# The last unit's last two gate tiles move from the pool that is replaced to the pool that stays

## The chip, the cores and the metric

The kernel runs on one core of a Trainium2 chip. The metric is the device time of one execution, in microseconds (us). The core has five engines that work side by side, each on its own queue in order: TensorE (PE in the profile, with its weight loads as PEld), VectorE (DVE), ScalarE (ACT), GpSimd (POOL) and SyncE (SP). Here SP issues the loads of the weights, and POOL issues most other DMA transfers. Tiles live in SBUF; matmuls write to PSUM.

## The reference

What is computed is an encoder trunk of two layers on 512 positions of 1024 channels. Each layer projects its normalized input once, for three branches and for a gate per branch, then merges, projects back and runs an MLP:

```python
for l in range(DEPTH):
    xn = rms_norm(x, ln1[l])
    z = xn @ w_in[l]
    a_q, a_i, a_ff, a_fb, a_g, b_u, b_v, c_q, c_k, c_v, gz = jnp.split(z, offsets, axis=-1)
    o_a = hgrn2_bidirectional(a_q, a_i, a_ff, a_fb, lower[l])
    ...
    y_b = spatial_gating(jax.nn.gelu(b_u), jax.nn.gelu(b_v), w_s[l], b_s[l])
    ...
    y_c = window_attention(qh, kh, vh, sink[l])
    gates = jax.nn.sigmoid(gz.reshape(bsz, s_len, N_BRANCH, D_MODEL))
    merged = (gates[:, :, 0] * (y_a @ w_br[l, 0]) + gates[:, :, 1] * (y_b @ w_br[l, 1])
              + gates[:, :, 2] * (y_c @ w_br[l, 2]))
    x = x + merged @ w_out[l]
    x = x + jnp.square(jax.nn.relu(rms_norm(x, ln2[l]) @ w_up[l])) @ w_down[l]
return rms_norm(x, final_norm)
```

Branch A is a gated linear recurrence in both directions, branch B mixes positions within blocks of 128 by a matrix `w_s` per group, branch C is attention in a window with rotary positions. All values are float32.

## The kernel before, in words

**Precision.** A product is made of three matmuls in the type fp32r: the high parts of both factors, and the high part of each with the low part of the other. So each 128x1024 piece of a weight goes through three steps: a DMA from DRAM into a raw tile (`wr`, or `wq` in the units), a cast by ACT at L224 (`wh`), and a subtraction by DVE at L225 (`wl`).

**The units.** In each layer three blocks of the input projection are done by Strassen's method, with seven products in place of eight (`seven`, L434). These are the units u = 0, 1, 2. Unit 0 makes the values of branch A and one input of branch B (`vt`, `bv`). Units 1 and 2 make gates: `on_gate(0)` and `on_gate(1)`. Within a unit the products run in the order 1, 2, 6, 7, 5, 4, 3, and each gives two tiles in PSUM (`gA`, `gB`, `gC`). As a product ends, `on` (L868) copies it to a tile `zt`, adds it to one, or, for the last, `P1653`, takes its tanh straight from PSUM (L875). A finished gate tile of 128x512, 256 KB, is written to a scratch tensor `thd` in DRAM by a DMA on POOL's queue (`keep`, L866) and read back much later, in the merge.

**The pools.** `zt` and the shifted inputs `xs` live in the pool `G`, the units' raw weights in the pool `wq`. Behind the units both are ended (L903, L904) and two others take their room: `Y1` (`yh`) and `br`, in which the attention stage has nearly all its tiles (`ex`, `at`, `key`, `qt`, `kt`, `yb`, the masks `am` and `cmask`). A tile of the new pool can be written only when the tiles of the old one that lay there have been read. The pool `sb` stays throughout. It holds, under the tag `l` with eight slots, tiles of several stages, and among them the four small tables `wst` (the mixing matrices), `bsb` (their bias), `cos` and `sin` (L918 to L922). The slots of a tag are given out in the order in which the program asks for tiles.

**The order.** The program does not fix the order of instructions on an engine by hand: a scheduler builds it from the order in the text, from priorities and from its own estimate of when each thing is ready. So a change of one tile's place can move instructions at other places.

**Behind the units** PE goes on with the projection `f` (L229 to L231: 24 matmuls for each 512 columns) and then `q`, while ACT and DVE start branch A: `key` (L622) and `qt` (L614) for the matmuls `at` (L600). Branch B comes in between: the matmuls `mx` (L944) multiply `wst` with `bv`, DVE adds `bsb` (`yb`, L947), multiplies by `bu` (L948), and ACT and DVE split the result (`yh`, L287, `yl`, L288). `mx` has two PSUM tiles in turn. Branch C later multiplies by `cos` and `sin`, which DVE first scales by the row norm (L989). In the first layer the mask `am` is loaded too, in two halves (L912), and cast to bytes by DVE (L913).

## Time and profile before

| | us |
|---|---|
| median of three runs | 1692.38 |
| lowest and highest of them | 1691.42, 1693.87 |
| the profiled execution | 1692.82 |
| its span | 1690.9 |
| outside the span | 1.9 |
| PE busy | 1675.8 |
| DVE busy | 1287.7 |
| ACT busy | 1010.1 |
| bytes moved by DMA | 195.83 MB, 116 GB/s on average |

The granted clock of TensorE is full (0.999) over the whole span. The span starts at 0 us; the units of the first layer end at 161.6 us, those of the second at 1003 us. In a row of the timeline the first number is the start, the second the duration, and in brackets stands how long the engine had been idle before and what ended that. In a row of waits stand the total, the number of times and the longest. In a row of DMA issues stand how many, the size of each, and the median time from issue to landing.

### The profile page before, as it was taken

The page shows a single profiled execution, that of the slowest core. Times are in us where ns is not written, and L with a number is a line of the kernel's source. Part 1 is how long each engine was busy: PE and PEld are TensorE (multiplying, and loading weights), DVE is VectorE, ACT ScalarE, POOL GpSimd, SP SyncE. Part 2 cuts the span into 40 slices and gives each one's busy share as a digit, 9 for nine tenths or more (in the row PEclk, how much of TensorE's full clock was granted, in tenths as well). Part 3 has the DMA queues.
Part 4 walks back from the last instruction along what each step waited for, and adds up shares of the span by engine and source line. Part 5 has one row for each costly group of instructions (what it writes and reads, how often), then busy time and mean ns, then how long its engine had stood idle before and what let it go on. Part 6 is the DMA issues. An engine that isn't in the chain of part 4 may idle for free.

```text
span 1690.9 us, 21905 instructions
## 1 busy us (share of the span) xinstructions
PE 1675.8 (99%) x8034; PEld 1403.3 (83%) x8034; DVE 1287.7 (76%) x2011; ACT 1010.1 (60%) x1714; POOL 111.0 (7%) x169
## 2 busy tenths in 40 slices
PE   9999999999999999999999999999999999999998
PEld 8888888888888888888788888888887888888886
DVE  7996998685656768686989869986846577585967
ACT  7566678765235554545765768698752355545464
POOL 1011000110200000000010110000002000000000
PEclk9999999999999999999999999999999999999999
DMA  8342222132645333332423422212227353232311
GB/s 326 112 149 88 89 77 69 57 113 94 227 153 187 100 100 100 100 109 91 137 91 122 161 92 76 99 44 88 94 81 252 129 186 100 100 113 87 125 63 50
DMA packets 58138, 195.83 MB, mean 116 GB/s; under 512 B 7504, under 2 KB 7888, under 8 KB 58032
## 3 DMA queue, kind: packets, MB, share of 16 engines
q1 hardware_dynamic: 47520, 160.23, 27.9%
q0 software_dynamic: 10368, 33.96, 5.7%
q8 instruction: 63, 1.03, 0.2%
q14 instruction: 43, 0.35, 0.1%
q10 hardware_dynamic: 144, 0.26, 0.0%
HBM read 175.54 MB, written 18.87 MB: 115 GB/s over the span
## 4 chain that ended last, share of the span: by engine, by line
PE 78%; DVE 9%; ACT 7%; issue 5%; DMA 1%; POOL 1%; POOLq 0%; DVEq 0%; ACTq 0%
PE up L229 7%; PE up L231 7%; PE up L230 7%; PE dA L447 3%; PE dA L445 3%; PE dA L446 3%; PE wo L280 2%; PE wo L281 2%; PE wo L279 2%; PE dC L446 2%; PE dC L445 2%; PE dC L447 2%; DVE ex L642 2%; PE at L600 1%; PE po L1084 1%
## 5 line engine op out<-in xcount | busy, mean ns | idle before, releaser
L224 ACT CAST wh<-wq 128x1024 fp32r<-128x1024 f32 x201 | 211.6, 1053 | 200.2 <-PE dA L446 48.3
L225 DVE TENSOR_TENSOR wl<-wq,wh 128x1024 fp32r<-128x1024 f32 x201 | 244.9, 1222 | 110.2 <-ACT wh L224 109.0
L225 DVE TENSOR_TENSOR wl<-wr,wh 128x1024 fp32r<-128x1024 f32 x166 | 203.5, 1226 | 142.3 <-ACT wh L224 135.7
L224 ACT CAST wh<-wr 128x1024 fp32r<-128x1024 f32 x166 | 174.2, 1050 | 223.3 <-PE up L230 73.4
L229 PE MATMUL up<-xh,wh 128*128 128x512 f32 x512 | 199.3, 389 | 0.0
L230 PE MATMUL up<-xl,wh 128*128 128x512 f32 x512 | 199.2, 389 | 0.0
L231 PE MATMUL up<-xh,wl 128*128 128x512 f32 x512 | 198.2, 389 | 0.0
L231 PEld LDWEIGHTS up<-xh,wl 128*128 128x128 f32 x512 | 96.1, 188 | 20.0
L230 PEld LDWEIGHTS up<-xl,wh 128*128 128x128 f32 x512 | 96.1, 188 | 19.9
L229 PEld LDWEIGHTS up<-xh,wh 128*128 128x128 f32 x512 | 96.1, 188 | 19.8
L445 PE MATMUL dA<-wh,sh 128*128 128x512 f32 x256 | 99.7, 389 | 0.0
L446 PE MATMUL dA<-wh,sh 128*128 128x512 f32 x256 | 99.6, 389 | 0.0
L447 PE MATMUL dA<-wl,sh 128*128 128x512 f32 x256 | 92.9, 389 | 0.0
L642 DVE TENSOR_TENSOR ex<-ex 128x512 f32<-128x512 f32 x112 | 74.8, 685 | 2.5 <-ACT key L622 2.4
L600 PE MATMUL at<-qt,kt 128*128 128x128 f32 x448 | 63.4, 275 | 1.7 <-ACT yh L287 1.7
L600 PEld LDWEIGHTS at<-qt,kt 128*128 128x128 f32 x448 | 58.5, 191 | 3.7 <-ACT yh L287 1.8
L614 ACT ACTIVATE qt<-ex 128x512 f32<-128x512 f32 x56 | 37.6, 672 | 35.2 <-DVE ex L642 19.8
L446 PEld LDWEIGHTS dA<-wh,sh 128*128 128x128 f32 x256 | 48.1, 188 | 10.0
L447 PEld LDWEIGHTS dA<-wl,sh 128*128 128x128 f32 x256 | 48.1, 188 | 9.9
L445 PEld LDWEIGHTS dA<-wh,sh 128*128 128x128 f32 x256 | 48.0, 188 | 9.9
L287 ACT CAST sh<-sf 128x512 fp32r<-128x512 f32 x64 | 39.7, 620 | 21.9 <-DVE sf L410 16.6
L230 PE MATMUL gz<-xl,wh 128*128 128x512 f32 x128 | 50.8, 397 | 0.0
(413 smaller groups left out, 4339.7 us busy)
## 6 DMA issues: line engine op xcount, KB each, us to landing
wr<-in_ws_dram SPq DMA_DIRECT2D x166, 512.0 KB, 3.3
wq<-in_ws_dram SPq DMA_DIRECT2D x117, 512.0 KB, 4.3
thd<-zt POOLq DMA_DIRECT2D x32, 256.0 KB, 2.5
th<-thd POOLq DMA_DIRECT2D x32, 256.0 KB, 3.1
mgd<-mg POOLq DMA_DIRECT2D x16, 256.0 KB, 2.3
mB<-mgd POOLq DMA_DIRECT2D x16, 256.0 KB, 4.6
xt<-in_xt_dram SPq DMA_DIRECT2D x8, 256.0 KB, 7.3
mcd<-th POOLq DMA_DIRECT2D x8, 256.0 KB, 3.4
```

The lines of the kernel that those rows point to most:

```text
L224: cast_i[0] = nc.scalar.copy(hi, raw)
L225: nc.vector.tensor_tensor(lo, raw, hi.bitcast(F32), ALU.subtract)
L229: nc.tensor.matmul(pt, whi, xhi, start=first, stop=False)
L230: nc.tensor.matmul(pt, whi, xlo, start=False, stop=False)
L231: return nc.tensor.matmul(pt, wlo, xhi, start=False, stop=last)
L287: nc.scalar.copy(hi, src)
L445: nc.tensor.matmul(pt, xh[:, t], hi[:, c], start=start and k == 0, stop=False, skip_group_check=True)
L446: nc.tensor.matmul(pt, xl[:, t], hi[:, c], start=False, stop=False, skip_group_check=True)
L447: return nc.tensor.matmul(pt, xh[:, t], lo[:, c], start=False, stop=k == 3, skip_group_check=True)
L600: nc.tensor.matmul(pt[:, c], kk(st), qq[:, c], start=True, stop=True)
L614: nc.scalar.activation(qt.rearrange(shp, b=nb, h=2), e_q, AF.Exp)
L642: nc.vector.tensor_tensor(o_ap, o_ap, ap_of(ex, i_, [[istep, 2]] + z), ALU.add)
```

## The change

The two tiles of the product `P1653` of the last unit (`i` is 1) are asked for under the tag `l`, which lies in the pool `sb`, and no longer under `zt`, which lies in the pool `G`. The unit before keeps `zt`. Nothing else in the text differs:

```diff
@@ -871,7 +871,7 @@
                     w[which, p] = T("zt", "zt")
                     A.copy(w[which, p], pt)
                 elif which == "P1653":
-                    z = T("zt", "zt")
+                    z = T("l" if i else "zt", "zt")
                     A.activation(z, pt, AF.Tanh, scale=sc[:, 4 + p:5 + p])
                     keep(z, p, 1)
                 else:
```

Both tiles are 128x512 in float32, and both tags hold such tiles. The four tables stand later in the program and take the slots of `l` behind the two tiles. Both kernels have the same instructions in number; their order differs between the first gate unit and the merge of each layer, and nowhere else.

POOL's queue in the first layer, one piece of the difference, at the end of the units (`zt_1217` and `zt_1219` are the tiles of the product before the last, `zt_1369` and `zt_1372` those of the last):

```order
 L866 DMA thd<-zt_1217 128x512
 L866 DMA thd<-zt_1219 128x512
+L919 DMA wst_1394<-in_wst_dram 128x512
+L920 DMA bsb_1395<-in_bsb_dram 128x512
 L866 DMA thd<-zt_1369 128x512
+L921 DMA cos_1396<-in_rope_dram 128x512
+L922 DMA sin_1397<-in_rope_dram 128x512
 L866 DMA thd<-zt_1372 128x512
 L916 DMA cmask_1392<-in_cmask_dram 128x384
```

Before, the four loads stood far ahead, in the first unit; now they stand among the last four gate tiles. The second layer has the same order.

PE's queue in the first layer, within the projection `f` behind the units, one piece of the difference (`mx_1579` and `mx_1587` are the first two groups of branch B's mixing, `at_1408` is branch A's first):

```order
 L229 MATMUL f_346_1668<-xh_189,wh_1664 128x512
+L944 MATMUL mx_1579<-wst_1394,bv_792 128x128
+L944 MATMUL mx_1579<-wst_1394,bv_794 128x128
+L600 MATMUL at_1408<-qt_1403,kt_1406 128x128 x4
+L944 MATMUL mx_1579<-wst_1394,bv_612 128x128
+L944 MATMUL mx_1579<-wst_1394,bv_614 128x128
+L944 MATMUL mx_1587<-wst_1394,bv_792 128x128
+L944 MATMUL mx_1587<-wst_1394,bv_794 128x128
+L944 MATMUL mx_1587<-wst_1394,bv_612 128x128
+L944 MATMUL mx_1587<-wst_1394,bv_614 128x128
 L230 MATMUL f_346_1668<-xl_190,wh_1664 128x512
```

The eight `mx` matmuls of the first two groups stood before in pairs at four places within the units; `at_1408` stood some 20 rows later, among the `mx` of the fourth group. The third group (`mx_1595`) now follows seven rows of `f`, two groups of `at` and one more row of `f`.

DVE's queue in the first layer at the same place. Before:

```order
L225 TENSOR_TENSOR wl_1706<-wr_1703,wh_1705 128x1024
L947 TENSOR_TENSOR yb_1584<-mx_1579,bsb_1395 128x512
L947 TENSOR_TENSOR yb_1592<-mx_1587,bsb_1395 128x512
L948 SCALAR_TENSOR_TENSOR bu_430<-yb_1584,bu_430 128x512
L788 TENSOR_TENSOR z_338_1629<-f_342_1636,rb_399 128x512
L948 SCALAR_TENSOR_TENSOR bu_432<-yb_1592,bu_432 128x512
L615 TENSOR_TENSOR qt_1403<-qt_1403,q_494 128x512
L642 TENSOR_TENSOR ex_1092<-ex_1092 128x2x256
L913 CAST amask_t<-am_1384 128x448
L913 CAST amask_t<-am_1387 128x448
```

And in the changed kernel, from the second row behind `wl_1706` on:

```order
L642 TENSOR_TENSOR ex_1092<-ex_1092 128x2x256
L913 CAST amask_t<-am_1384 128x448
L913 CAST amask_t<-am_1387 128x448
L642 TENSOR_TENSOR ex_1092<-ex_1092 128x2x256
L788 TENSOR_TENSOR z_338_1629<-f_342_1636,rb_399 128x512
L225 TENSOR_TENSOR wl_1739<-wr_1736,wh_1738 128x1024
L615 TENSOR_TENSOR qt_1425<-qt_1425,q_494 128x512
L642 TENSOR_TENSOR ex_1092<-ex_1092 128x2x128x2
L989 TENSOR_TENSOR cos_1396<-cos_1396,rb_399 128x512
L642 TENSOR_TENSOR ex_1092<-ex_1092 128x2x128x2
L989 TENSOR_TENSOR sin_1397<-sin_1397,rb_399 128x512
L947 TENSOR_TENSOR yb_1584<-mx_1579,bsb_1395 128x512
```

`yb` was first behind the last `wl` of the units; now branch A's first steps, the two casts of `am` and the two products of `cos` and `sin`, which stood in the first unit before, come ahead of it. On SP's queue the two loads of `am` now stand ahead of the third weight load behind the units (`wr_1773`), and not behind it.

## The prediction

> **What bounds the kernel now.** I read the page first, for the engine that is full.

> ```profile
> PE 1675.8 (99%) x8034; PEld 1403.3 (83%) x8034; DVE 1287.7 (76%) x2011; ACT 1010.1 (60%) x1714; POOL 111.0 (7%) x169
> ```

> TensorE is the bound: 1675.8 of 1690.9 us. The change removes no instruction, so it can gain only what TensorE waits, 15.1 us in all, and of that only what lies where the order of work differs: about 100 to 425 us (first layer) and 925 to 1273 us (second). So next the view of waits, for PE alone, in these two stretches:

> ```profile
> PE at L600 <- ACT yh L287: 1.7, 1, 1.7
> PE pT L1079 <- ACT yc L1086: 0.9, 1, 0.9
> ...
> PE po L1084 <- ACT pT L1080: 0.6, 1, 0.6
> PE kT L657 <- ACT at L620: 0.6, 1, 0.6
> PE f L229 <- DVE gz L967: 0.4, 1, 0.4
> PE gA L445 <- ACT wh L224: 0.3, 1, 0.3
> PE pT L1079 <- ACT yc L1086: 0.2, 1, 0.2
> PE yC L279 <- DVE mC L1147: 0.2, 1, 0.2
> ```

> The first two are the first layer, the other six the second: 2.6 + 2.3 = 4.9 us. This is the most that better order can bring here. The first, 1.7 us, is the one at the edit. The timelines of PE, ACT, DVE, POOL and SP around it (start, us, what; in brackets the idle time before and who ended it), and last the chain of waits:

> ```profile
> 161.61 0.39 PE L229 MATMUL f<-xh,wh 128*128 128x512 f32 x1
> ...
> 170.91 1.72 PE L944 MATMUL mx<-wst,bv 128*128 128x128 f32 x14
> 174.31 0.46 PE L600 MATMUL at<-qt,kt 128*128 128x128 f32 x2 [1.68 <-ACT yh L287]
> ...
> 162.57 1.05 ACT L224 CAST wh<-wr 128x1024 fp32r<-128x1024 f32 x1
> 169.28 1.06 ACT L622 ACTIVATE key<-ex 128x1024 f32<-128x1024 f32 x1 [5.66 <-DMA thd<-zt]
> ...
> 169.35 1.29 DVE L947 TENSOR_TENSOR yb<-mx,bsb 128x512 f32<-128x512 f32 x2 [4.47 <-DMA thd<-zt]
> ...
> 158.17 1.16 POOL L866 DMA_DIRECT2D thd<-zt  x2 [4.34 <-ACT zt L881]
> 162.12 1.22 POOL L866 DMA_DIRECT2D thd<-zt  x2 [2.79 <-ACT zt L875]
> ...
> 158.54 6.69 SPq L200 DMA_DIRECT2D wr<-in_ws_dram  x3
> 169.23 0.81 SPq L912 DMA_DIRECT2D am<-in_amask_dram  x2
> ...
> 162.80 6.18 DMA thd<-zt
> ```

> The units' last product (gA) ends where f begins, at 161.61. The last two gate tiles are issued to DRAM at 162.12 and 162.7, and the second lands 6.2 us after its issue, at 168.98; until then ACT, DVE, POOL and SP all stand, because their next instructions write into the pool that replaces the one where these tiles lie. TensorE lives on 41 matmuls of f (161.61 to 170.91, 0.227 us each) and the mx matmuls, and then runs dry for 1.68 us: mx needs yb to empty its PSUM tile, the at matmuls need qt.

> **The change part by part.**

> *The wait that goes.* In the new order the attention stage waits for the tiles of the product before (issued at 158.17 and 158.7) and no longer for the last two. The transfers issued from 158.0 to 159.5 landed in:

> ```profile
> thd<-zt POOLq DMA_DIRECT2D x2, 256.0 KB, 3.5
> ```

> So the wait ends near 162 us, not at 168.98. The key instruction of ACT is then released not by the transfer but by the cast at 162.57: it can start some 5 us sooner than 169.28. Thus qt, issued as the second after it, is ready near 165. If nothing else is late, the whole 1.68 us gap goes.

> *What is moved into its place.* wst, bsb, cos and sin take slots of the tag "l" behind the two tiles, and are now issued among the last gate tiles. The first of them today:

> ```profile
> wst<-in_wst_dram POOLq DMA_DIRECT2D x1, 256.0 KB, 3.0
> ```

> All four are issued from 38 us on, where nothing waits for them, and cost nothing. Now 4 x 256 KB = 1 MB comes into the busiest stretch. In turn the mx matmuls that stood in the units, 8 in each layer, move behind f's 34th matmul:

> ```profile
> 106.28 0.60 PE L944 MATMUL mx<-wst,bv 128*128 128x128 f32 x4
> 106.64 0.71 PE L447 MATMUL gA<-wl,xs 128*128 128x512 f32 x2
> 107.19 0.39 PE L445 MATMUL gA<-wh,xs 128*128 128x512 f32 x1
> ```

> From 106.28 to 107.19 are 0.91 us, of which the two gA matmuls take 2 x 0.227, so two mx matmuls (four rows) cost 0.457 us; eight are 1.83 us. TensorE works as much as before: the units end 1.83 us sooner (gA at 159.8) and f's stretch is 1.83 us longer. There are ten switches fewer between the two number formats on PE (302, not 312); since mx rows take 0.114 us there and 0.123 us in the block of 14 at 170.91 (1.72/14), I price them at nothing to 0.1 us and take 0.1.

> *Does wst come in time?* PE reaches the first mx 34 x 0.227 = 7.7 us after 159.8, at 167.5. wst is issued behind the transfer of 156.9 (158.7 less 1.83), near 157.5. The stretch's own prices are:

> ```profile
> wr<-in_ws_dram SPq DMA_DIRECT2D x3, 512.0 KB, 5.3
> thd<-zt POOLq DMA_DIRECT2D x4, 256.0 KB, 5.3
> am<-in_amask_dram SPq DMA_DIRECT2D x2, 224.0 KB, 2.6
> ```

> At 5.3 us it lands by 162.8, with 4.7 us to spare. Price: zero; without this cover each us is one on the path.

> *The tightest link: am.* In DVE's new queue the two casts of am stand ahead of both cos and sin products and of yb; yb frees the PSUM that mx's second half needs. PE gets there after 34 f matmuls (167.5), eight mx (1.83), three groups of at (0.94 each, from the 16 rows in 2.04 us below), and eight f matmuls (1.8): 174.0.

> ```profile
> 174.31 2.04 PE at L600 x16
> 173.43 0.68 DVE L615 TENSOR_TENSOR qt<-qt,q 128x512 f32<-128x512 f32 x1
> 174.03 0.68 DVE L642 TENSOR_TENSOR ex<-ex 128x512 f32<-128x512 f32 x1
> 174.63 0.68 DVE L913 CAST amask_t<-am 128x448 uint8<-128x448 f32 x2
> 175.24 1.21 DVE L225 TENSOR_TENSOR wl<-wr,wh 128x1024 fp32r<-128x1024 f32 x1
> ```

> From am's landing to the end of the first yb DVE has the two casts (0.61), seven products of 128x512 at a pitch of 0.60 (4.2), the wl (1.13) and yb itself (0.68): 6.6 us. So am must land by 167.4. It is issued when gA's end (159.8) and the earlier gate tiles (160.5 to 161) have cleared, so it has 6.4 to 6.9 us. Lower bound of its landing: the 2.6 us of today, a stall of nothing. Upper: all that is under way then.

> ```profile
> 160.00:165.00 5.00, 5.00 (x23) 4.13 (x22) 2.45 (x2) 2.42 (x3) 1.08 (x2) 1.00 0.87 291
> ```

> The last three numbers are the granted clock, the share of the DMA engines and GB/s: in this stretch they are 87% busy at 291 GB/s, about 334 if full. On SP's own queue some 1.1 MB go up to am's end (the rest of one wr, another wr, am). If SP's and POOL's queues halve the rate, that takes 1.1 MB / 167 GB/s = 6.6 us, landing near 167.5 with a little for the start. If am waits for every byte under way, 2.0 to 2.6 MB at 291 GB/s, it takes 7 to 9 us: 168 to 170. I take a stall of 0.5 us, near the first (one wr of 512 KB takes 5.3 us here, and so do the gate tiles, which go in pairs of 512 KB: neither queue is preferred), with 0 and 2.6 as ends. [...]

> *cos and sin* are needed by DVE at about 171; issued near 161, they have 10 us. POOL's queue holds wst, bsb, tile, cos, sin, tile, cmask: at 167 GB/s its six times 256 KB and 192 KB from 157.5 on take 10.6 us, so sin comes before 167 and cmask last, which this row needs first at 226 us:

> ```profile
> L1053 DVE CUSTOM_DVE_ANT_0 sc<-sc,cmask,snk_t x64: 462/544/619, 225.6 to 1232.8; 128x256 f32<-128x256 f32 x32, 128x384 f32<-128x384 f32 x32
> ```

> Both cost nothing.

> *The second layer* loses and gains nothing at this place:

> ```profile
> 1005.00:1010.00 5.00, 5.00 (x24) 4.14 (x23) 2.35 (x3) 1.64 (x3) 0.54 (x1) 1.00 0.78 285
> ...
> ACT qt L614 <- DMA thd<-zt: 3.4, 1, 3.4
> ```

> ACT waits 3.4 us for the tiles there too, but PE never stops: it has no am in the way and more matmuls in hand. f still has wst some 3 us ahead of its need.

> *The other gaps* (0.92 and the 2.3 us of layer 2) come from ACT's order among small steps. DVE has 24 to 25 of 25 us in use from 175 to 250, so its sooner start (some 3 us after the 1.4 us for cos and sin that now fall here) may clear the 0.92; a new order can as well make gaps of 0.2 to 0.9. I put their sum at zero, with -3.2 and +1.5 as ends.

> **Sum:** -1.68 + 0.5 - 0.1 = -1.3 us. Profiled execution 1692.8 to 1691.5; it stood 0.4 above the median of 1692.38, so the median goes to 1691.1.

> **The rivals.**

> A, *the sooner start carries on*: the transition's gap goes whole and the small gaps of the reordered stretches with it. For it: DVE is full behind the transition and gets 3 us ahead. Against: the second layer's gaps are ACT's and lie 100 us and more behind. 4.9 us less at most, three quarters of it likely: 1692.4 - 3.8 = 1688.6.

> B, *the wait only changes its name*: am, or the wr in front of it, comes 1.2 us later than I put it, and PE's 1.68 us stand at mx in place of at. For it: 1 MB more in a stretch with the engines 87% busy. Against: half the rate suffices. 1692.3.

> C, *slower: the late loads hold DVE's queue*. One mechanism: the am casts hold all that stands behind them on DVE, cos, sin and yb, and PE stands at mx's second half. It decides from a landing of am at 169.1 (1.68 us past 167.4). What the engines moved from 157 to 170 us, and the gate tiles' landing over the whole run:

> ```profile
> DMA packets 754, 2.65 MB, mean 204 GB/s; under 512 B 112, under 2 KB 112, under 8 KB 752
> ...
> thd<-zt POOLq DMA_DIRECT2D x32, 256.0 KB, 2.5
> ```

> With all 2.6 MB ahead of it at this mean it takes 12.7 us from 161: 173.7, a stall of 6.3, net +4.6; at 291 GB/s 9 us, net +0.9. The middle: 1695.1. [...]

> **How the numbers follow.** Forecast 0.43, A 0.18, B 0.22, C 0.17. The time is the forecast's, 1691.1, its own range 1690.0 to 1692.0. The whole range goes from 1688.0 (all but A's last us) to 1694.8 (half of C), leaving out some 0.15. About 0.2%, 3.4 us, is what a measurement tells from no change: faster than 1689.0 is most of A and a little of the forecast's tail, 0.16; slower than 1695.8 some half of C with new gaps added, 0.11; the rest, 0.73, is the same.

> **What would show it.** Right: ACT's key starts by 164, behind a cast and not behind thd; no gap ahead of at; a gap under 1 us, if any, ahead of the mx matmuls of the third tile, behind DVE; am landing 6 to 7 us after issue; units ending 1.8 us sooner in both layers. B shows a gap of 1.2 to 2.2 us at that mx, C of over 2; A shows none there and none at pT near 272. Wrong altogether: PE stopping at the first mx for wst, new gaps over 1 us in the second layer, or a time outside 1688.0 to 1694.8.

## The result, and the profile after

The changed kernel is slower: 1694.78 us (1692.68 to 1696.54, 20 executions) beside 1691.79 us of the kernel before (1690.48 to 1693.87, 20 executions). The ratio is 1.0018, with a 95% interval of 1.0011 to 1.0024. The forecast was 1691.1, within 1690.0 to 1692.0.

The page of the changed kernel, first line of the engines:

```profile
PE 1677.9 (99%) x8034; PEld 1404.5 (83%) x8034; DVE 1291.1 (76%) x2011; ACT 1010.8 (60%) x1714; POOL 111.7 (7%) x169
```

TensorE does the same 8034 matmuls and is busy 2.1 us longer. The waits of PE in the two stretches where the order differs, first layer, then second:

```profile
PE at L600 <- DVE qt L615: 2.3, 1, 2.3
PE mx L944 <- DVE yb L947: 1.0, 1, 1.0
...
PE at L600 <- ACT on L701: 1.4, 1, 1.4
PE f L229 <- DVE gz L967: 0.4, 1, 0.4
PE gz L229 <- DVE gz L967: 0.2, 1, 0.2
```

In the first layer 3.3 us stand where 2.6 stood, at other places; in the second 2.0 where 2.3 stood. The timelines of PE, ACT, DVE and SP behind the units of the first layer show what happened:

```profile
167.10 0.60 PE L944 MATMUL mx<-wst,bv 128*128 128x128 f32 x4
167.54 1.06 PE L600 MATMUL at<-qt,kt 128*128 128x128 f32 x8
...
171.38 1.05 PE L600 MATMUL at<-q,key 128*128 128x128 f32 x8
174.72 1.49 PE L600 MATMUL at<-qt,kt 128*128 128x128 f32 x8 [2.29 <-DVE qt L615]
...
177.64 3.78 PE L944 MATMUL mx<-wst,bv 128*128 128x128 f32 x16 [1.01 <-DVE yb L947]
...
161.65 1.06 ACT L622 ACTIVATE key<-ex 128x1024 f32<-128x1024 f32 x1
...
168.91 0.39 DVE L913 CAST amask_t<-am 128x448 uint8<-128x448 f32 x1 [3.60 <-DMA am<-in_amask_dram]
171.24 0.39 DVE L913 CAST amask_t<-am 128x448 uint8<-128x448 f32 x1 [1.94 <-DMA am<-in_amask_dram]
...
173.89 0.69 DVE L615 TENSOR_TENSOR qt<-qt,q 128x512 f32<-128x512 f32 x1
...
162.09 1.02 SPq L912 DMA_DIRECT2D am<-in_amask_dram  x2
```

The edit does what it says: `key` starts at 161.65 and not at 169.28, and the first two `at` groups wait for nothing. But DVE's queue comes to the casts of `am` at 165.3 and stands there for 5.5 us, since the two halves land only at 168.9 and 171.2. Behind them stand the `qt` of the third `at` group and `yb`, and PE waits for both.

The second thing is in the column of the granted clock (the third number from the end):

```profile
174.00:175.00 1.00, 0.28 (x2) 0.32 (x3) 1.00 (x2) 0.05 (x1) 0.00 (x0) 1.00 0.01 4
175.00:175.50 0.50, 0.50 (x6) 0.50 (x5) 0.50 (x2) 0.00 (x0) 0.00 (x0) 0.83 0.70 205
175.50:176.00 0.50, 0.50 (x5) 0.50 (x3) 0.50 (x2) 0.00 (x0) 0.00 (x0) 0.50 0.93 360
177.00:178.00 1.00, 0.36 (x1) 0.36 (x2) 1.00 (x2) 0.56 (x2) 0.00 (x0) 0.50 0.00 0
178.00:180.00 2.00, 2.00 (x11) 2.00 (x11) 2.00 (x5) 0.59 (x1) 0.00 (x0) 0.50 0.00 0
180.00:182.00 2.00, 2.00 (x9) 1.88 (x9) 2.00 (x4) 0.76 (x3) 0.00 (x0) 0.50 0.00 0
182.00:182.50 0.50, 0.50 (x3) 0.38 (x2) 0.50 (x2) 0.50 (x2) 0.00 (x0) 0.84 0.00 0
```

From 175.33 to 182.16 us, 6.8 us long, TensorE ran at half its clock (the two ends follow from the means 0.83 and 0.84 of the half microseconds in which they lie). The 16 rows of `mx` took 3.78 us in it; at the full clock the same 16 rows take 1.95 us (a row of the run with `am` on POOL, below).

The executions of the changed kernel are not alike in this. Of the 31 of two series (20 and 11), sorted by their mean granted clock:

| mean clock | executions | mean time, us | from, to |
|---|---|---|---|
| 0.999 | 7 | 1693.78 | 1692.68, 1694.40 |
| 0.998 | 11 | 1694.32 | 1693.74, 1696.14 |
| 0.997 and 0.996 | 13 | 1695.93 | 1695.17, 1696.68 |

So the executions with the highest mean clock are 2.0 us above the kernel before, and those with the lowest 4.1. The mean is a rough sign of a fall only, since the end of the span is at half clock as well, behind PE's last rows: the last 4.9 us in the profile of the kernel before (from 1686.08 us on, so its clock is not full over the whole span), the last 2.9 us in the first one of the changed kernel (from 1690.85).

### The profile page after: what moved, and what is told of

Same layout as the page of the kernel before. It is cut to its first block, busy times and chain, and to the rows that moved or that the text cites. A ratio compares the mean times of both kernels' runs of the same rounds, so it can differ in the third digit from the quotient of the medians.

```text
span 1693.7 us, 21890 instructions
## 1 busy us (share of the span) xinstructions
PE 1677.9 (99%) x8034; PEld 1404.5 (83%) x8034; DVE 1291.1 (76%) x2011; ACT 1010.8 (60%) x1714; POOL 111.7 (7%) x169
## 4 chain that ended last, share of the span: by engine, by line
PE 92%; issue 2%; ACT 2%; DMA 1%; DVE 1%; POOL 0%; POOLq 0%; SPq 0%; ACTq 0%; DVEq 0%
PE up L230 7%; PE up L229 7%; PE up L231 7%; PE dA L445 3%; PE dA L446 3%; PE dA L447 3%; PE at L600 3%; PE po L1084 2%; PE wo L280 2%; PE wo L281 2%; PE wo L279 2%; PE dC L445 2%; PE dC L446 2%; PE dC L447 2%; PE gz L229 2%
## 5 line engine op out<-in xcount | busy, mean ns | idle before, releaser
L224 ACT CAST wh<-wq 128x1024 fp32r<-128x1024 f32 x201 | 211.6, 1053 | 199.7 <-PE up L230 47.4
L225 DVE TENSOR_TENSOR wl<-wq,wh 128x1024 fp32r<-128x1024 f32 x201 | 245.2, 1223 | 108.8 <-ACT wh L224 107.5
L224 ACT CAST wh<-wr 128x1024 fp32r<-128x1024 f32 x166 | 174.2, 1050 | 245.6 <-PE up L230 71.3
L225 DVE TENSOR_TENSOR wl<-wr,wh 128x1024 fp32r<-128x1024 f32 x166 | 203.9, 1229 | 142.2 <-ACT wh L224 135.8
L229 PE MATMUL up<-xh,wh 128*128 128x512 f32 x512 | 199.3, 389 | 0.0
L229 PEld LDWEIGHTS up<-xh,wh 128*128 128x128 f32 x512 | 96.1, 188 | 19.9
L445 PE MATMUL dA<-wh,sh 128*128 128x512 f32 x256 | 99.7, 389 | 0.0
L447 PE MATMUL dA<-wl,sh 128*128 128x512 f32 x256 | 92.9, 389 | 0.0
L642 DVE TENSOR_TENSOR ex<-ex 128x512 f32<-128x512 f32 x112 | 76.0, 697 | 2.2 <-ACT key L622 2.0
L600 PE MATMUL at<-qt,kt 128*128 128x128 f32 x448 | 63.3, 276 | 3.7 <-DVE qt L615 2.3
L600 PEld LDWEIGHTS at<-qt,kt 128*128 128x128 f32 x448 | 58.5, 192 | 6.2 <-ACT at L620 2.4
L447 PEld LDWEIGHTS dA<-wl,sh 128*128 128x128 f32 x256 | 48.1, 188 | 10.0
L445 PEld LDWEIGHTS dA<-wh,sh 128*128 128x128 f32 x256 | 48.1, 188 | 9.9
L614 ACT ACTIVATE qt<-ex 128x512 f32<-128x512 f32 x56 | 37.6, 672 | 25.8 <-DVE ex L642 22.2
L287 ACT CAST sh<-sf 128x512 fp32r<-128x512 f32 x64 | 39.6, 620 | 21.9 <-DVE sf L410 16.6
L229 PE MATMUL gz<-xh,wh 128*128 128x512 f32 x128 | 50.8, 397 | 0.2 <-DVE gz L967 0.2
## 6 DMA issues: line engine op xcount, KB each, us to landing
wr<-in_ws_dram SPq DMA_DIRECT2D x166, 512.0 KB, 3.3
wq<-in_ws_dram SPq DMA_DIRECT2D x117, 512.0 KB, 4.3
thd<-zt POOLq DMA_DIRECT2D x32, 256.0 KB, 2.6
th<-thd POOLq DMA_DIRECT2D x32, 256.0 KB, 3.1
mgd<-mg POOLq DMA_DIRECT2D x16, 256.0 KB, 2.8
mB<-mgd POOLq DMA_DIRECT2D x16, 256.0 KB, 5.3
xt<-in_xt_dram SPq DMA_DIRECT2D x8, 256.0 KB, 7.3
mcd<-th POOLq DMA_DIRECT2D x8, 256.0 KB, 3.1
```

The source lines that it names most:

```text
L224: cast_i[0] = nc.scalar.copy(hi, raw)
L225: nc.vector.tensor_tensor(lo, raw, hi.bitcast(F32), ALU.subtract)
L229: nc.tensor.matmul(pt, whi, xhi, start=first, stop=False)
L287: nc.scalar.copy(hi, src)
L445: nc.tensor.matmul(pt, xh[:, t], hi[:, c], start=start and k == 0, stop=False, skip_group_check=True)
L447: return nc.tensor.matmul(pt, xh[:, t], lo[:, c], start=False, stop=k == 3, skip_group_check=True)
```

## The experiments

The theory after the result: **am holds DVE's queue, and the waits this makes let the clock fall.** `am` is late because a megabyte of tables is now loaded ahead of it and beside it. The rivals: the new order is bad as such; the loads slow everything; the sooner start only brings the next wait.

### One layer at a time

```diff
-                    z = T("l" if i else "zt", "zt")
+                    z = T("l" if i and l == 0 else "zt", "zt")
```

> The change in the first layer only; the second layer's order is that of the kernel before. Theory (am holds DVE's queue, and the TensorE waits that follow let the granted clock fall): the whole loss is here. Some 2.5 to 4 us slower than before (1694.3 to 1695.8 beside 1691.8), PE waits of about 2.3 us at at (behind DVE qt) and 1.0 us at mx (behind DVE yb) as in the changed kernel's profile, and executions with a clock of 0.999 and others of 0.996 to 0.998. Rival (the moved loads and the new order cost a little at both layers): about half the loss, 1693.3, clock 0.999.

Measured: 1696.2 us, ratio 1.0023 (1.0014 to 1.0031), 0.4 us above the expected range. With `l == 1` instead:

> The change in the second layer only, where no am is loaded. Theory: no loss, 1691.3 to 1692.2 beside 1691.8 (the waits of the second layer were 2.3 us before and 2.0 us after the change), clock 0.999 in all executions. Rival (loss at both layers): about 1693.3.

Measured: 1690.4 us, ratio 0.9994 (0.9985 to 1.0003), clock 0.998 to 0.999; this is 0.9 us below the expected range. The whole loss is in the first layer, the only one with `am`; the second layer alone loses nothing and may gain a little. The waits of PE with the first layer alone, and that layer's timeline:

```profile
PE at L600 <- DVE qt L615: 1.8, 1, 1.8
PE mx L944 <- DVE yb L947: 1.6, 1, 1.6
...
169.24 0.39 DVE L913 CAST amask_t<-am 128x448 uint8<-128x448 f32 x1 [3.78 <-DMA am<-in_amask_dram]
170.91 0.39 DVE L913 CAST amask_t<-am 128x448 uint8<-128x448 f32 x1 [1.28 <-DMA am<-in_amask_dram]
```

The same pair of waits, 3.4 us in sum, behind the same casts.

### Another engine waits for am

```diff
-                nc.vector.tensor_copy(amask_t[:, w], am[:, 0:448])
+                nc.gpsimd.tensor_copy(amask_t[:, w], am[:, 0:448])
```

> The change, but am is cast to bytes by POOL instead of DVE: the four tables are loaded as late as in the changed kernel and am lands as late, only nothing of DVE's queue stands behind it but the masked copy at L605. Theory (it is am at the head of DVE's queue): the two PE waits in the first layer shrink from 3.3 us to under 0.5 us, the clock stays 0.999, and the time is 1690.0 to 1691.0, 1 to 2 us below before. Rival (the moved megabyte slows every load, and other waits take over): at least one PE wait of over 1.5 us remains in the first layer, 1693 or more.

Measured: 1688.87 us (1688.46 to 1689.81), ratio 0.9983 (0.9974 to 0.9991): faster than the kernel before, 5.9 us below the changed one, and 1.1 us below the expected range. The transfer is nearly as late as in the changed kernel, but now POOL waits for it, with nothing urgent behind. POOL's and PE's timelines:

```profile
170.03 0.65 POOL L913 CAST amask_t<-am 128x448 uint8<-128x448 f32 x1 [4.59 <-DMA am<-in_amask_dram]
171.64 0.61 POOL L913 CAST amask_t<-am 128x448 uint8<-128x448 f32 x1 [0.96 <-DMA am<-in_amask_dram]
...
172.72 1.05 PE L600 MATMUL at<-q,key 128*128 128x128 f32 x8
173.60 1.06 PE L600 MATMUL at<-qt,kt 128*128 128x128 f32 x8
...
174.73 1.95 PE L944 MATMUL mx<-wst,bv 128*128 128x128 f32 x16
```

POOL waits 5.6 us for `am`; the third `at` group and the `mx` rows follow without a gap, and the clock is full (1.00) from 174 to 186 us. PE's rows from the first `f` row behind the units to about 195 us stand in the same order as in the changed kernel, and DVE's too up to `yb`, but for the two casts. So neither the moved loads nor the new order cost anything themselves here; that DVE stood in line for `am` did. The gain over the kernel before is in the waits of PE: 1.8 us in the two stretches, all in the second layer, beside 4.9, and a span of 1688.0 us beside 1690.9.

### The cast on POOL without the change

The same edit in the kernel before.

> The kernel before with one edit: am is cast by POOL and not by DVE. The two gate tiles stay in the pool that is replaced. Theory (the sooner start of the attention stage is what the kernel gains once am is out of the way): the 1.7 us wait at at stays, 1691.0 to 1692.0. Rival (the cast on DVE was the cost all along, also in the kernel before): the wait goes, 1689.5 or less.

Measured: 1691.82 us, ratio 1.0003 (0.9994 to 1.0012). The cast was no cost in the kernel before, so the 2.9 us of the run above come from the two edits together. The time is as expected, but not the wait at `at`: it was not 1.7 us in this execution. Its row, and the one of the run with the second layer alone, whose first layer is that of the kernel before:

```profile
172.77 1.13 PE L600 MATMUL at<-qt,kt 128*128 128x128 f32 x8 [0.48 <-ACT yh L287]
```

```profile
173.29 1.13 PE L600 MATMUL at<-qt,kt 128*128 128x128 f32 x8 [0.62 <-ACT yh L287]
```

The last gate tiles landed sooner there (median 4.7 and 4.8 us for the four, not 5.3). The 1.68 us from which the prediction started is the longest of three such waits, 0.5, 0.6 and 1.7 us.

### The tables early, the start early

The four tables take their slots ahead of the two tiles (shortened; the lines further down that asked for the tables and loaded them are left out of the kernel):

```diff
+        tables = lambda: [...]  # the four T("l", ...) and their DMAs
         for u in range(3):
-            nxt = uload(l, "un", u + 1) if u < 2 else None
+            nxt = uload(...); wst_t, bsb_t, cos_t, sin_t = tables() if u == 2 else [None] * 4
```

> The change, but wst, bsb, cos and sin are asked for ahead of the last unit, so that they take their slots before the two tiles do and are loaded in the first unit as in the kernel before. The attention stage keeps its earlier start. Without the two tiles' new place this reordering of the text gives exactly the order of before. Theory (the loss comes from the moved loads ahead of am, the earlier start itself is a gain): the 1.7 us wait at at is gone and nothing takes its place, 1689.7 to 1690.7, clock 0.999. Rival 1 (any start sooner only brings the next wait): 1691.3 to 1692.3. Rival 2 (the new order itself is bad): 1693 or more.

Measured: 1690.87 us, ratio 0.9995 (0.9986 to 1.0004). The loss is gone; the time is just above the expected range, and the gain of 0.9 us is not clear of nothing. `am`, from the view of its tile:

```profile
L912 SPq DMA_DIRECT2D am<-in_amask_dram x2: 328/390/451, 163.5 to 163.9; - x2
L913 DVE CAST amask_t<-am x2: 383/388/394, 169.5 to 169.9; 128x448 uint8<-128x448 f32 x2
...
DMA to landing us min/median/max: 5.1/5.5/5.9
```

Its halves land 5.1 and 5.9 us after issue, at 168.6 and 169.8, and DVE comes to their casts at 169.5 and 169.9: just in time, without a wait. In the first layer 0.4 us of waits are left, in the second 2.6.

### Half of the loads

Only `cos` and `sin` are asked for early; `wst` and `bsb`, half a megabyte, still come late.

> The change, with cos and sin asked for ahead of the two tiles, so that half a megabyte (wst, bsb) and not a whole one is loaded at the end of the units. In DVE's queue the casts of am stand at the same place. Theory (the bytes under way decide when am lands): am lands some 1.5 us sooner than in the changed kernel (168.9 and 171.2 us), the PE waits of the first layer come to 1 to 2.2 us and not 3.3, the clock stays at 0.999 in most executions, 1690.8 to 1692.5. Rival (any load there costs the whole): 1694 or more.

Measured: 1692.39 us, ratio 1.0004 (0.9995 to 1.0012). DVE's row and the landing from the view of the tile; behind them the same lines of the changed kernel's view:

```profile
168.88 0.90 DVE L913 CAST amask_t<-am 128x448 uint8<-128x448 f32 x2 [2.94 <-DMA am<-in_amask_dram]
...
DMA to landing us min/median/max: 6.1/6.2/6.2
```

```profile
DMA to landing us min/median/max: 6.8/7.8/8.7
```

The landing goes from 5.5 us (no table late) over 6.2 (half) to 7.8 (all), medians of the two halves of `am`. The second half, which held DVE until 171.2, now lands with the first, and the first layer's waits are 0.7 and 0.3 us. That the time still is that of the kernel before was not separated. In the second layer this order has 3.0 us of waits beside 2.3, and PE's order in the first layer is a little different too, so the size is a rough one.

### Both mends together

The tables early and `am` on POOL.

> Both mends together: the four tables take their slots before the two tiles and are loaded early, and am is cast by POOL. Theory (each mend alone takes the am wait away from the end; together they have nothing left to gain): as with the tables early alone, 1689.8 to 1691.2. Rival (the moved loads still cost something where am is cast by POOL): 1688.4 or less.

Measured: 1691.47 us, ratio 1.0000 (0.9991 to 1.0009), slightly above the expected range. Nothing is gained by the second mend, as the theory says; the time is no better than with the tables early alone, and clearly behind the late tables with `am` on POOL. In the profiles the difference is in the waits of PE, 3.9 us here (1.1 of them at `pT` in the first layer) beside 1.8 with the late tables, at spans of 1690.4 and 1688.0 us. Why this order has them was not separated: the orders differ in both layers.

### Filling the wait

The matmuls of the second `at` group are done three times, ahead of the third group, to keep TensorE busy in the wait (one line of the edit; in the helper `attn` the third group's first row is ordered behind the added ones):

```diff
-                pt = attn(lambda st: dg[:, st * P:(st + 1) * P], q)
+                pt = attn(lambda st: dg[:, st * P:(st + 1) * P], q, 3 if l == 0 and h == 0 else 1)
```

> The changed kernel with work added: in the first layer the eight rows of the second at group (q times key) are done three times, the same values into the same PSUM tile, ahead of the third group, where TensorE waited 2.3 us. Nothing else on the way to the end is touched: DVE and the loads are as in the changed kernel. Theory (a wait of 2 to 3 us lets the granted clock fall to one half, which costs up to 3 us more): the added 1.9 us fill the wait, the clock of TensorE stays 1.00 in 175 to 182 us, and the kernel is 1 to 2.5 us faster than the changed one, 1692.3 to 1693.8 beside 1691.8 of the kernel before. Rival (the waits alone are the loss and the clock has no part): 1694.8 or, as far as the wait is shorter in some executions, up to 1 us more.

Measured: 1696.99 us, ratio 1.0029 (1.0018 to 1.0040), 2.2 us slower than the changed kernel, and above the range of the rival too. The half of the theory on the clock held: it stayed full in the profile (below) and at 0.998 to 0.999 in all seven executions. The time did not follow. PE's waits show the most of why:

```profile
PE mx L944 <- DVE yb L947: 1.8, 1, 1.8
...
PE gz L229 <- DVE mx L1055: 1.0, 1, 1.0
PE vT L1025 <- DVE cv L779: 0.3, 1, 0.3
...
178.00:182.00 4.00, 4.00 (x26) 3.61 (x27) 4.00 (x8) 1.76 (x3) 0.00 (x0) 1.00 0.00 0
```

The 16 added rows moved a row of `f` from ahead of `mx` to behind it, so that wait grew to 1.8, and new waits for DVE came up later, 1.0 us at `gz` and 0.3 at `vT`; from 172 to 194 us DVE is busy without a break here. With the first wait filled the clock stayed up in this run (1.00 from 165 to 194 us). For the whole time it is no measure of what the clock costs, since the work added changed the order behind it. But up to the first row of the next projection, `ck`, PE's work is that of the changed kernel and the 16 added rows, and there the filled wait is ahead: PE took 161.5 us from the first `f` row of the layer to it, beside 163.1 in the first profile of the changed kernel. What was won was lost behind that row.

### The same kernel again

For that cost stand further profiles of the changed kernel itself.

> The changed kernel itself once more, for executions in which the clock falls and executions in which it does not. Theory: an execution whose mean clock is 0.999 takes 1692.5 to 1693.6 us, one with 0.996 or 0.997 takes 1695.3 to 1696.5; what lies between is 3.4 or 6.8 us at half clock in 175 to 182 us of the first layer, and the waits are alike in both. Rival (the clock only goes along with longer waits, which are the loss): the profile of an execution without the fall shows PE waits that are shorter by the whole difference.

> The changed kernel once more, one look, for a second profile to lay beside the others: with the clock falling, or not, as said of the run before.

> The changed kernel once more, for an execution in which the clock does not fall. Theory: the clock falls where one of its windows of 3.4 us is idle by more than half (2.0 to 2.4 us of PE waits in the three profiles with a fall, 1.8 us in one without), so by chance of where the windows lie, in some half of the executions. Without the fall the waits at at and at mx are there all the same, 2.3 us and, since PE reaches mx sooner, 1.3 to 1.6 us; PE then runs ahead of DVE, which is full from 175 to 250 us, so further waits of 1 to 2 us appear there, and the execution takes 1693.5 to 1694.5 us, 2 us and not 3 below one with the fall. Rival (shorter waits): 1 us or less in sum at the two places.

> As the run before: one more look at the changed kernel, with the clock falling (then 1695.3 to 1696.6 us and 6.8 us at half clock) or not (then 1693.5 to 1694.5 us and more waits between 180 and 250 us).

Measured: 1694.40 us (11 executions), ratio 1.0015 (1.0006 to 1.0024), then one execution each of 1696.56, 1695.70 and 1696.59. In the series of 11 the two executions at 0.999 took 1694.02 and 1694.40, above the 1692.5 to 1693.6 expected of them; the four at 0.996 and 0.997 took 1695.17 to 1696.68, near the 1695.3 to 1696.5. All four profiles had a fall, so an execution of this kernel without one was never seen in detail; the waits of 1 to 2 us that were expected there between 180 and 250 us stay open. But in the execution of 1695.70 (clock 0.998) it fell for only one stretch of 3.4 us, later than in the others. Its stretches, with the clock again third from the end:

```profile
174.00:178.00 4.00, 1.37 (x9) 1.08 (x9) 4.00 (x7) 1.65 (x4) 0.00 (x0) 1.00 0.40 131
178.00:178.75 0.75, 0.04 (x1) 0.04 (x1) 0.75 (x3) 0.64 (x2) 0.00 (x0) 0.84 0.00 0
178.75:181.50 2.75, 2.75 (x13) 2.75 (x14) 2.75 (x5) 0.62 (x1) 0.00 (x0) 0.50 0.00 0
181.50:182.00 0.50, 0.50 (x4) 0.50 (x4) 0.50 (x2) 0.30 (x1) 0.00 (x0) 0.57 0.00 0
```

Its PE waits in the first layer are the longest of all:

```profile
175.80 1.13 PE L600 MATMUL at<-qt,kt 128*128 128x128 f32 x8 [2.59 <-DVE qt L615]
...
178.71 3.57 PE L944 MATMUL mx<-wst,bv 128*128 128x128 f32 x16 [1.55 <-DVE yb L947]
```

What the clock costs can be read at the first row of `ck`, which PE reaches some 190 us into the span. Counted from the first `f` row of the layer, so that the start of the execution has no part (for the last line of the table the time at half clock is worked out from the lengths of its rows of `at`, `mx` and `f`):

| run | at half clock, us | waits at `at` and `mx`, us | to `ck`, us | beyond 156.7, less the waits, us |
|---|---|---|---|---|
| `am` on POOL | none | none | 156.7 | |
| the filled wait, with 1.8 us of added rows | none | 2.2 | 161.5 | 0.8 (less the added rows too) |
| changed, 1695.70 | 3.4 | 4.1 | 162.8 | 2.0 |
| changed, first profile | 6.8 | 3.3 | 163.1 | 3.2 |
| changed, the other three | 6.8 | 3.6, 3.6, 3.8 | 163.4, 163.5, 163.6 | 3.1, 3.2, 3.1 |

The execution with the longest waits and the shortest fall reaches `ck` first of the five. So the rival, by which a lower clock only goes along with longer waits, does not hold: 6.8 us at half clock cost 2.3 to 3.2 us here and 3.4 us cost 1.2 to 2.0, the lower figures with the 0.8 us taken off that the filled wait shows without a fall. Where these 0.8 us come from is open. The waits that come from `am` vary by themselves: 3.3 to 4.1 us in sum over the five profiles of the changed kernel.

## Why the prediction was wrong

**What held.** The gap at `at` behind the gate tiles goes; `key` starts behind a cast, as predicted by 164 us; `wst` is in time (issued at 157.1, landed within 4.8 us, first used at 167.1 without a wait); `cos`, `sin` and `cmask` cost nothing; the second layer neither gains nor loses much. The units of the first layer, counted from the first `f` row, end 1.4 us sooner, where 1.8 was forecast. DVE's queue behind `am` was named as the tightest link, and the outcome is nearest to rival C, the casts of `am` holding DVE's queue, which was given 0.17. That C's middle, 1695.1, lies so near the measured 1694.8 is in part luck: it is made of stalls of 2.6 to 6.3 us and no fall of the clock, and the runs show a stall of 3.3 and a fall in many executions. C's sign was a gap of over 2 us at `mx`; there stood 1.0, and 2.3 at `at`, which no rival named.

**The step that failed is the landing of am, and with it the size of its stall**, 0.5 us in the sum, 3.3 in the first profile. By the prediction's own limit, 167.4, the landing measured would have given 3.8. Two parts of the landing were off, and the place of the wait:

- *The issue.* It was put at 160.5 to 161, from gate tiles that land 3.5 us after issue. With the tables behind them the second of the two took 4.7 us, from 156.6 to 161.3. By the profile SP waited for it 1.9 us, and `am` was issued at 162.09.
- *The landing.* It was taken as one transfer of 6.6 us, with SP's and POOL's queues at half of the rate each; that was an estimate, and no run shows the share of each queue for `am` alone. The halves took 6.8 and 8.7 us. The first is right; the second was the one that counted, since DVE does nothing between the casts. That is 168.9 and 171.2 us against 167.5. The bytes under way were priced with the rows of the kernel before, 2.65 MB from 157 to 170 us; in the changed kernel it was this:

```profile
DMA packets 1392, 4.25 MB, mean 327 GB/s; under 512 B 217, under 2 KB 469, under 8 KB 1390
```

- *Who waits first.* The prediction asked when `mx` of the third group needs `yb` (174.0). The third `at` group stands ahead of it on PE, and its `qt` stands on DVE behind the same casts: it was due at 172.4. The 2.3 us stood there, and only 1.0 us at `mx`. This moved the place of the wait and not its sum.

The bound at 2.6 us of stall was a bound of landing at 170 us, too low by 1.2 us, for the same second half.

**The price of the old wait** was taken from one execution, 1.68 us, where the two other profiles with this first layer (in one of them `am` is cast on POOL) show 0.5 and 0.6. That execution took 1692.82 us, 1 us above the median of the 20 executions, 1691.79. So less was to be won at that place than the sum said. With `am` out of the way more was won than the 1.3 us forecast, 2.9, since the 0.9 us at `pT` and part of the second layer's waits went too. That is what rival A said of a start that carries on, and its time, 1688.6, is near the 1688.87 of that run.

**The clock is a term that the prediction does not have.** It priced an idle us as one us. The clock was full up to the end of PE's work (1.00 up to 1686.08 us), and the 1.68 us gap of the kernel before leaves it full, so no row of before showed the cost. By the table above a fall of 6.8 us costs 2.3 to 3.2 us. A second sum for the profile of the changed kernel: PE begins the last transposes ahead of the second layer with this row before, and this one after:

```profile
844.18 0.80 PE L353 MATMUL xT<-id_t,xr 128*128 128x128 f32 x4 [0.91 <-ACT u L358]
```

```profile
847.29 0.80 PE L353 MATMUL xT<-id_t,xr 128*128 128x128 f32 x4 [0.91 <-ACT u L358]
```

That is 3.1 us later; the first `f` row began 0.8 us sooner in this execution (27.07 beside 27.89), so the first layer is 3.9 us longer. The waits give 0.7 (3.3 less 2.6). The 16 `mx` rows at half clock give 1.8 (3.78 less 1.95). The `at` rows of 174.72 give 0.4 (1.49 less 1.05), and three rows of `f` at 181.07 to 182.35 some 0.6 (1.28 less 3 x 0.227). Together 3.5 of 3.9; the rest is in single rows that were not summed. Over executions, those with a mean clock of 0.997 or less took 2.1 us longer than those with 0.999 (1695.93 less 1693.78); their waits are not on record, so this difference is not the clock's alone for certain.

## What to carry to other kernels

The two casts that waited for a late transfer held everything behind them on their engine, for 5.5 us: ask of each load that a change moves into a busy stretch which instruction waits for it, and put that on an engine with nothing urgent behind it. Here, with the two tiles moved, one word, `gpsimd` for `vector`, turned a loss of 3 us into a gain of 2.9. And where a transfer comes in pieces, ask when the last one lands: here it was at 171.2 us, and the first at 168.9. Take the price of a wait from several executions, not from one.

## What the runs showed of the hardware

In this kernel, in which TensorE is busy for 99% of the span, 2.0 to 2.6 us without work for it were followed by a clock of one half, for 3.4 or 6.8 us, and that cost 1.2 to 3.2 us more (the table above).

Laid over the waits, the stretches of this grid that ended in a fall were idle for 2.0, 2.1, 2.3, 2.4, 2.5 and 2.6 us (in the last three the place of the fall is worked out from the lengths of the rows). In four of the six it was one gap, of 2.3 to 2.6 us; in the other two it was the parts of two gaps (1.8 and 1.6 us, 2.6 and 1.5 us) that lay in one stretch. For example, in the execution of 1695.70 the stretch from 175.10 to 178.52 holds 0.70 us of the wait that ends at 175.80 and 1.36 of the one that begins at 177.16. Stretches that did not end in a fall were idle for 1.9 us (the stretch before that one, 171.69 to 175.10, holds the rest of the first wait) and 1.3 (the kernel before, whose step at 1686.08 puts another 443 pieces ahead of it, at 173.97). The run with the filled wait, with waits of 0.2 and 1.8 us there, shows no step by which its grid could be laid. So here 1.9 us, 55% of a stretch, left the clock full, and 2.0 us, 60%, did not; and where a gap lay on the grid made a difference: the one of 2.6 us in the execution of 1695.70, parted by a step into 1.9 and 0.7, did not bring a fall alone. Of 31 executions of the changed kernel 13 show a mean clock of 0.997 or less.
